# Channel-major projections and gates: three 256-column matmuls into the same PSUM columns, where a 512- and a 256-column one wrote two halves that were added later

## The chip, the core and the metric

The kernel runs on one core of a Trainium2 chip. The metric is the device time of one execution in microseconds. Of three runs before the change the median is 1530.15 us (1529.57 to 1530.34).

The engines that matter are TensorE (PE in the profile; PEld is its weight load), VectorE (DVE), ScalarE (ACT), GpSimd (POOL) and SyncE (SP), which issues most DMAs. A matmul has a stationary operand, loaded ahead of it by a weight load of its own, and a moving operand that streams through column by column; its result is added up in PSUM.

## What is computed

Two layers, each an RMSNorm, one input projection of 2048 features, two mixers side by side (an mLSTM and a gated linear recurrence), and an output projection that is added to x; a last RMSNorm stands at the end. Sequence 256, all in float32. Cut to the parts that the change touches:

```python
u = rms_norm(x, norm_g)
p = u @ w_in
qk, v, o, z_a, ig, fg, xb, z_b = jnp.split(p, SPLIT_AT, axis=-1)
qk = jax.nn.silu(causal_dwconv(qk, qk_conv))
...
xc = causal_dwconv(xb, lru_conv_w) + lru_conv_b
y_b = rg_lru(xc, w_a, b_a, w_x, b_x, lam) * jax.nn.silu(z_b)
...
r = sigmoid(einsum("bshi,hij->bshj", xh, w_a) + b_a)
i = sigmoid(einsum("bshi,hij->bshj", xh, w_x) + b_x)
```

## The kernel before

**Numbers in two parts.** A float32 operand is split into a high part H in a reduced format (fp32r) and the rest L, and a product a b is taken as aH bH + aL bH + aH bL. For the weights, `prepare` does this for every block of 128 x 1024: a ScalarE cast (line 222, tile wH) and a VectorE subtraction (through the helper at line 111, tile wL). The normalised x is kept transposed in x_s as [128, 16 feature tiles, 2 parts, 256 tokens], so that high and low part of one feature tile lie side by side.

**Two forms of projection.** The chunks o, v and z and the output projection are token-major (`mm_a`, lines 238 to 240): stationary is a 128-token slice of x or y, moving is a weight block of 512 columns, three matmuls for the three products into the same PSUM columns. The chunks qk, xb and zb are channel-major (`mm_b`): stationary is a 128 x 128 block of weights, moving is x_s. Here line 255 moves both parts of x_s at once, 512 columns, against wH, so that the product with the high part lands in columns 0 to 255 and that with the low part in columns 256 to 511; line 257 moves the high part against wL and adds into columns 256 to 511. The two halves are added on the way out of PSUM. The gates w_a and w_x (`gate_half`, lines 595 and 597) do the same with xcs, the split output of the convolution.

**On the way out.** `evac_b` copies the first half (ScalarE, line 329), adds the second (VectorE) and multiplies by the norm factor rb (VectorE) into padt (qk, xb: 32 times) or zb (16 times). In the gates ScalarE adds the bias to one half (line 601), VectorE adds the other, and one Sigmoid of 1024 columns follows (line 604).

**Order.** `_plan` lists chunks by layer and group of heads (two layers, four groups). Each chunk is cut into halves of one weight block; the last loop of `tile_trunk` walks over the halves, prepares weights three halves ahead (`AHEAD`), emits the half's matmuls and then pumps background work (convolutions, mLSTM steps, scans) from generators. `pump` stops when its credit is used up; every piece of work takes its estimated cost from the credit, `evac_b` 1.2. A scheduler then settles the order on each engine, by what buffers and operands allow. In PSUM there are two acc tiles of [128, 2, 512] for the projections, and four 512-column buffers (`aux`) that ps_gt (gates), ps_S, ps_n (mLSTM), ps_ty (transposes) and ps_g share. The mLSTM steps use the helper `mm3` (lines 428 to 430), and `gates_mm` (lines 353 and 354) makes the 16 input and forget gate columns into ps_g, once a layer.

Of the kernel before, what the change touches and what calls it, by code (L numbers as in the profile page):

```python
# [9 lines left out]
F32 = mybir.dt.float32  # L10
F32R = mybir.dt.float32r
AF = mybir.ActivationFunctionType
ALU = mybir.AluOpType
# [3 lines left out]
P = 128  # L17
D = 2048
T = 256
# [29 lines left out]
def tile_trunk(ctx, tc, x, xt, par, gw, gb, ws, final_g, out):  # L49
    nc = tc.nc  # L50
    V, S, G, PE = nc.vector, nc.scalar, nc.gpsimd, nc.tensor
# [8 lines left out]
    ps_main = ctx.enter_context(tc.tile_pool(name="ps_main", bufs=2, space=PSUM))  # L60
    ps_aux = ctx.enter_context(tc.tile_pool(name="ps_aux", bufs=4, space=PSUM))

    def aux(name):
        return ps_aux.tile([P, 512], F32, tag="aux", name=name)
# [9 lines left out]
    pars = const.tile([P, DEPTH, NPAR], F32, name="pars")  # L74
# [35 lines left out]
    def tt_(o, a, b, op):  # L110
        return V.tensor_tensor(out=o, in0=a, in1=b, op=op)  # L111

    def stt(o, a, s, b, op0, op1):
        return V.scalar_tensor_tensor(out=o, in0=a, scalar=s, in1=b, op0=op0, op1=op1)

    def ts_(o, a, s1, op0, s2=None, op1=None):
        if s2 is None:
            return V.tensor_scalar(out=o, in0=a, scalar1=s1, scalar2=None, op0=op0)
        return V.tensor_scalar(out=o, in0=a, scalar1=s1, scalar2=s2, op0=op0, op1=op1)

    def log1p_exp_half(x_, tl):
        """returns q with log1p(exp(-|x|)) = 2 q"""
        z = tl("z")
        stt(z, x_, -1.0, x_, ALU.mult, ALU.min)
        S.activation(out=z, in_=z, func=AF.Exp)
        d = tl("d")
        ts_(d, z, 2.0, ALU.add)
        V.reciprocal(out=d, in_=d)
        s = tl("s")
        tt_(s, z, d, ALU.mult)  # L130
        s2 = z
        tt_(s2, s, s, ALU.mult)
        p = d
        ts_(p, s2, 1.0 / 15, ALU.mult)
        for c in (13, 11, 9, 7, 5, 3):
            stt(p, p, 1.0 / c, s2, ALU.add, ALU.mult)
        stt(p, p, 1.0, s, ALU.add, ALU.mult)
        return p
# [47 lines left out]
    halves = []  # L186
    st = {"nload": 0, "credit": 0.0}
# [15 lines left out]
    def add_unit(mms, before=None, after=None):  # L203
        box = {}
        for i in range(2):
            halves.append(dict(box=box, i=i, mm=mms[i], split=None,
                               before=before if i == 0 else None, after=after if i == 1 else None))
# [35 lines left out]
    def mm_b(acc, k0, first, last):  # L243
        def f(H, L):
            Hv = H.rearrange("p (k c) -> p k c", k=4)
            Lv = L.rearrange("p (k c) -> p k c", k=4)
            ps = acc()
            xs = st["x"]
            for k in range(4):
                kt = k0 + k  # L250
                for ct in range(2):
                    csl = slice(P * ct, P * ct + P)
                    s = first and k == 0
                    e = last and k == 3
                    PE.matmul(ps[:, ct, :], Hv[:, k, csl], xs[:, kt].rearrange("p a t -> p (a t)"),  # L255
                              start=s, stop=False, skip_group_check=True)
                    PE.matmul(ps[:, ct, T : 2 * T], Lv[:, k, csl], xs[:, kt, 0, :], start=False, stop=e,  # L257
                              skip_group_check=True)
        return f

    def chunk_in(l, kind, g, postfn, beforefn=None):
        def make_acc():
            box = {}

            def acc():
                if "t" not in box:
                    box["t"] = ps_main.tile([P, 2, 512], F32, tag="acc", name="acc")
                return box["t"]
            return acc

        if kind in ("qk", "xb", "zb"):
            for s_ in range(2):
                acc = make_acc()
                for u in range(2):
                    mms = [mm_b(acc, 8 * u + 4 * i, u == 0 and i == 0, u == 1 and i == 1) for i in range(2)]
                    add_unit(mms, after=(lambda acc=acc, s_=s_: postfn(acc(), s_)) if u == 1 else None)
        else:
            acc = make_acc()
            for u in range(4):
                mms = [mm_a(acc, lambda: st["x"][:, :, 0], lambda: st["x"][:, :, 1], 4 * u + 2 * i,  # L280
                            u == 0 and i == 0, u == 3 and i == 1) for i in range(2)]
                add_unit(mms, before=beforefn if u == 0 else None,
                         after=(lambda: postfn(acc())) if u == 3 else None)

    def bc(ap2, n):
        return ap2.unsqueeze(1).to_broadcast([P, n, T])
# [39 lines left out]

    def evac_b(l, o, acc):
        require(("rb", l))
        S.copy(out=o, in_=acc[:, :, 0:T])
        tt_(o, o, acc[:, :, T : 2 * T], ALU.add)  # L330
        tt_(o, o, bc(st["rb", l], 2), ALU.mult)
        st["credit"] -= 1.2

    def evac_pad(l, acc):
        padt = work.tile([P, 2, 260], F32, tag="pad", name="padt", bufs=2)
# [21 lines left out]
    def gates_gen(l):  # L357
# [13 lines left out]
        tt_(gi, gi, t_, ALU.add)  # L371
        yield 0.6
        q = log1p_exp_half(x_, sc)
        yield 4
        ts_(q, q, -2.0, ALU.mult)
# [207 lines left out]
    def gate_half(l, g, which):  # L583
        def f(H, L):
            xc, xs = st["xc", l, g]
            Hv = H.rearrange("p (b c) -> p b c", b=4)
            Lv = L.rearrange("p (b c) -> p b c", b=4)
            o_t = work.tile([P, 4, T], F32, tag="sA" if which == 0 else "sB", name=f"gate{which}")
            for b in range(2):
                for j in range(2):  # L590
                    ps = aux("ps_gt")
                    jl = slice(P * j, P * j + P)
                    for i in range(2):
                        ib = 2 * b + i
                        PE.matmul(ps, Hv[:, ib, jl], xs[:, ib].rearrange("p a t -> p (a t)"), start=i == 0,  # L595
                                  stop=False, skip_group_check=True)
                        PE.matmul(ps[:, T : 2 * T], Lv[:, ib, jl], xs[:, ib, 0, :], start=False, stop=i == 1,  # L597
                                  skip_group_check=True)
                    ct = 2 * b + j
                    off = (O_BA if which == 0 else O_BX) + 4 * g + ct  # L600
                    S.activation(out=o_t[:, ct, :], in_=ps[:, T : 2 * T], func=AF.Identity,
                                 bias=pars[:, l, off : off + 1])
                    tt_(o_t[:, ct, :], o_t[:, ct, :], ps[:, 0:T], ALU.add)
            st["sig"] = S.activation(out=o_t, in_=o_t, func=AF.Sigmoid)
            st["gate", which] = o_t
        return f

# [239 lines left out]
    for item in _plan():  # L847
        if item[0] == "in":
            emit_in(*item[1:])
        elif item[0] == "gate":  # L850
            _, l, g = item
# [21 lines left out]

# [1 line left out]
def _units():  # L875
    """the weight blocks in the order in which the kernel streams them: two halves a unit"""
    sl = lambda a, n: slice(a, a + n)
    units = []

    def chunk(l, kind, g):  # L880
        if kind in ("qk", "xb", "zb"):
            for s in range(2):
                if kind == "qk":
                    cs = [sl(256 * g + 128 * s, 128), sl(1024 + 256 * g + 128 * s, 128)]
                else:
                    cs = [sl((C_XB if kind == "xb" else C_ZB) + 512 * g + 256 * s, 256)]
                for u in range(2):
                    units.append([("w_in", l, (sl(1024 * u + 512 * i, 512), cs)) for i in range(2)])
        else:
            cs = [sl({"v": C_V, "o": C_O, "z": C_Z}[kind] + 512 * g, 512)]  # L890
            for u in range(4):
                units.append([("w_in", l, (sl(512 * u + 256 * i, 256), cs)) for i in range(2)])

    def out(l, g, c):
        for src in range(2):
            units.append([("w_out", l, (sl(2048 * src + 512 * g + 256 * i, 256), [sl(512 * c, 512)]))
                          for i in range(2)])

    for item in _plan():
        if item[0] == "in":  # L900
            chunk(*item[1:])
        elif item[0] == "gate":
            _, l, g = item
            units.append([(w, l, sl(2 * g, 2)) for w in ("w_a", "w_x")])
        elif item[0] == "out":
            out(*item[1:])
        else:
            _, l, g = item
            for kp in range(4):
                rows = sl(2048 * (kp // 2) + 512 * g + 256 * (kp % 2), 256)  # L910
                for c in (0, 2):
                    units.append([("w_out", l, (rows, [sl(512 * (c + i), 512)])) for i in range(2)])
    return units
# [52 lines left out]
```

## Time and profile before

| | |
|---|---|
| median of three runs | 1530.15 us |
| span of the profiled execution, first to last instruction | 1528.4 us |
| mean granted TensorE clock | 0.997 |
| VectorE, casts' subtractions (line 111, wL) | 643.8 us busy, 529 instructions |
| ScalarE, casts (line 222, wH) | 554.0 us busy, 529 instructions |
| mean DMA rate | 188 GB/s |

Times of the profile belong to one profiled execution, and count from its first instruction; its span is the time that the profile has for it, and the runs' times include a little more around it. A row of a group gives line, engine, operation, tiles (out<-in), shapes and count, then the busy time in us, the mean ns of one, and the idle time of the engine before them. A row of the timeline gives the start and the duration in us, then the same names. A duration of a matmul or a weight load reaches into the next one's.

### The profile page before, as it was taken

To read this page: it belongs to the slowest core of one execution; us is meant where nothing else is said; L and a number is where in the kernel's file an instruction comes from. 1 tells how busy PE (TensorE), PEld (TensorE's weight loads), DVE (VectorE), ACT (ScalarE), POOL (GpSimd) and SP (SyncE) were. 2 spreads that over 40 slices of the span, in tenths; PEclk is the share of its full clock that TensorE was granted. 3 is DMA by queue.
4 is the path that set the end of the run, shared out by engine and by line. 5 is a ranking of instruction groups with operands and counts; after the bars stand their busy time and mean duration, and the time that the engine had idled before them with its cause. 6 is when DMAs were issued, how large, how long until landed. Compare 5 with 4: busy or idle time off the path is not lost.

```text
span 1528.4 us, 19659 instructions
## 1 busy us (share of the span) xinstructions
PE 1510.9 (99%) x7576; PEld 1278.2 (84%) x7576; DVE 1127.6 (74%) x1594; ACT 885.4 (58%) x1141; POOL 37.6 (2%) x109
## 2 busy tenths in 40 slices
PE   8999999999999999999999999999999999999997
PEld 6888888888888888888888888888888888888885
DVE  6888867794677847778658787777847887478874
ACT  7567654674547645575555485557544575444854
POOL 0000100000000000000000001000000000000002
PEclk9999999999999999999999999999999999999998
DMA  9554655455554555445555555545555455555562
GB/s 344 192 188 164 212 185 182 173 196 194 188 190 171 191 193 193 175 183 193 175 184 180 190 176 193 193 173 192 193 193 185 173 184 197 187 182 187 171 223 102
DMA packets 45117, 288.03 MB, mean 188 GB/s; under 512 B 5072, under 2 KB 7648, under 8 KB 11744
## 3 DMA queue, kind: packets, MB, share of 16 engines
q1 hardware_dynamic: 43600, 283.40, 52.4%
q0 software_dynamic: 992, 3.16, 0.7%
q8 instruction: 59, 0.97, 0.3%
q14 instruction: 34, 0.28, 0.1%
q10 hardware_dynamic: 432, 0.23, 0.0%
HBM read 284.66 MB, written 2.11 MB: 188 GB/s over the span
## 4 chain that ended last, share of the span: by engine, by line
PE 98%; ACT 1%; DMA 0%; DVE 0%; SPq 0%; issue 0%; ACTq 0%
PE acc L255 24%; PE acc L238 18%; PE acc L240 18%; PE acc L239 18%; PE acc L257 12%; PE ps_gt L595 2%; PE ps_gt L597 1%; PE acc L788 0%; PE acc L790 0%; PE acc L789 0%; PE ps_ty L551 0%; DMA raw<-in_ws_dram 0%; PE acc_x L790 0%; PE acc_x L788 0%; PE acc_x L789 0%; PE ps_n L428 0%
## 5 line engine op out<-in xcount | busy, mean ns | idle before, releaser
L222 ACT CAST wH<-raw 128x1024 fp32r<-128x1024 f32 (+1 forms) x529 | 554.0, 1049 | 567.6 <-PE acc L240 282.6
L111 DVE TENSOR_TENSOR wL<-raw,wH 128x1024 fp32r<-128x1024 f32 (+1 forms) x529 | 643.8, 1220 | 312.3 <-ACT wH L222 311.5
L255 PE MATMUL acc<-x_s,wH 128*128 128x512 f32 x1536 | 544.1, 399 | 0.0
L257 PE MATMUL acc<-x_s,wL 128*128 128x256 f32 x1536 | 431.2, 281 | 0.0
L255 PEld LDWEIGHTS acc<-x_s,wH 128*128 128x128 f32 x1536 | 288.6, 188 | 71.0
L238 PE MATMUL acc<-wH,x_s 128*128 128x512 f32 x768 | 301.0, 392 | 6.7 <-ACT wH L222 6.7
L239 PE MATMUL acc<-wL,x_s 128*128 128x512 f32 x768 | 300.2, 391 | 0.3 <-DVE wL L111 0.3
L240 PE MATMUL acc<-wH,x_s 128*128 128x512 f32 x768 | 299.8, 390 | 0.0
L257 PEld LDWEIGHTS acc<-x_s,wL 128*128 128x128 f32 x1536 | 290.1, 189 | 0.9
L238 PEld LDWEIGHTS acc<-wH,x_s 128*128 128x128 f32 x768 | 144.7, 188 | 36.2 <-ACT wH L222 6.7
L239 PEld LDWEIGHTS acc<-wL,x_s 128*128 128x128 f32 x768 | 144.7, 188 | 30.3 <-DVE wL L111 1.2
L240 PEld LDWEIGHTS acc<-wH,x_s 128*128 128x128 f32 x768 | 144.6, 188 | 30.1
L238 PE MATMUL acc<-wH,ybH 128*128 128x512 f32 x224 | 88.1, 393 | 0.0
L238 PE MATMUL acc<-wH,yaH 128*128 128x512 f32 x224 | 87.8, 392 | 0.0
L239 PE MATMUL acc<-wL,yaH 128*128 128x512 f32 x224 | 87.4, 390 | 0.0
L240 PE MATMUL acc<-wH,yaL 128*128 128x512 f32 x224 | 87.4, 390 | 0.0
L240 PE MATMUL acc<-wH,ybL 128*128 128x512 f32 x224 | 87.3, 390 | 0.0
L239 PE MATMUL acc<-wL,ybH 128*128 128x512 f32 x224 | 87.2, 389 | 0.0
L238 PEld LDWEIGHTS acc<-wH,yaH 128*128 128x128 f32 x224 | 42.0, 188 | 9.1
L240 PEld LDWEIGHTS acc<-wH,yaL 128*128 128x128 f32 x224 | 42.1, 188 | 8.9
L240 PEld LDWEIGHTS acc<-wH,ybL 128*128 128x128 f32 x224 | 42.0, 188 | 8.8
L238 PEld LDWEIGHTS acc<-wH,ybH 128*128 128x128 f32 x224 | 42.1, 188 | 8.4
(201 smaller groups left out, 1437.2 us busy)
## 6 DMA issues: line engine op xcount, KB each, us to landing
raw<-in_ws_dram SPq DMA_DIRECT2D x260, 1024.0 KB, 4.8
raw<-in_ws_dram SPq DMA_DIRECT2D x6, 512.0 KB, 7.9
xp<-in_xt_dram SPq DMA_DIRECT2D x8, 256.0 KB, 7.4
x_acc<-in_x_dram SPq DMA_DIRECT2D x4, 512.0 KB, 9.7
nb<-nG_d POOLq DMA_DIRECT2D x8, 256.0 KB, 3.7
out_dram<-x_acc SPq DMA_DIRECT2D x8, 256.0 KB, 3.0
raw<-in_ws_dram SPq DMA_DIRECT2D x4, 256.0 KB, 6.3
fg<-in_final_g_dram POOLq DMA_DIRECT2D x2, 512.0 KB, 4.5
```

The source lines that it names most:

```text
L111: return V.tensor_tensor(out=o, in0=a, in1=b, op=op)
L222: S.copy(out=H[:, o : o + w], in_=r[:, o : o + w])
L238: PE.matmul(ps[:, t, :], a_H[:, kt, tsl], Hv[:, k, :], start=s, stop=False)
L239: PE.matmul(ps[:, t, :], a_H[:, kt, tsl], Lv[:, k, :], start=False, stop=False)
L240: PE.matmul(ps[:, t, :], a_L[:, kt, tsl], Hv[:, k, :], start=False, stop=e)
L255: PE.matmul(ps[:, ct, :], Hv[:, k, csl], xs[:, kt].rearrange("p a t -> p (a t)"), start=s, stop=False, skip_group_check=True)
L257: PE.matmul(ps[:, ct, T : 2 * T], Lv[:, k, csl], xs[:, kt, 0, :], start=False, stop=e, skip_group_check=True)
L595: PE.matmul(ps, Hv[:, ib, jl], xs[:, ib].rearrange("p a t -> p (a t)"), start=i == 0, stop=False, skip_group_check=True)
L597: PE.matmul(ps[:, T : 2 * T], Lv[:, ib, jl], xs[:, ib, 0, :], start=False, stop=i == 1, skip_group_check=True)
```

## The change

In `mm_b` and `gate_half` the matmul of 512 columns is cut in two of 256, and all three write to the same 256 columns. The two channel tiles of a chunk, which had a PSUM bank each, share one, so only the very first matmul into the bank clears it. `evac_b` multiplies straight from PSUM. In the gates a buffer holds two channel tiles, and the Sigmoid takes its input from PSUM with the bias. The cost that `evac_b` takes from the credit goes from 1.2 to 0.7.

```diff
@@ mm_b
-                    PE.matmul(ps[:, ct, :], Hv[:, k, csl], xs[:, kt].rearrange("p a t -> p (a t)"),
-                              start=s, stop=False, skip_group_check=True)
-                    PE.matmul(ps[:, ct, T : 2 * T], Lv[:, k, csl], xs[:, kt, 0, :], start=False, stop=e,
-                              skip_group_check=True)
+                    o = ps[:, ct, :]
+                    PE.matmul(o, Hv[:, k, csl], xs[:, kt, 0, :], start=s and ct == 0, stop=False, skip_group_check=True)
+                    PE.matmul(o, Hv[:, k, csl], xs[:, kt, 1, :], start=False, stop=False, skip_group_check=True)
+                    PE.matmul(o, Lv[:, k, csl], xs[:, kt, 0, :], start=False, stop=e, skip_group_check=True)
@@ chunk_in
+        def make_acc_b():
+            box = {}
+
+            def acc():
+                if "t" not in box:
+                    t = ps_main.tile([P, 2, 512], F32, tag="acc", name="acc")
+                    box["t"] = t[:, 0, :].rearrange("p (a t) -> p a t", a=2)
+                return box["t"]
+            return acc
+
...
-                acc = make_acc()
+                acc = make_acc_b()
@@ evac_b
-        S.copy(out=o, in_=acc[:, :, 0:T])
-        tt_(o, o, acc[:, :, T : 2 * T], ALU.add)
-        tt_(o, o, bc(st["rb", l], 2), ALU.mult)
-        st["credit"] -= 1.2
+        tt_(o, acc, bc(st["rb", l], 2), ALU.mult)
+        st["credit"] -= 0.7
@@ gate_half
+                ps = aux("ps_gt").rearrange("p (j t) -> p j t", j=2)
                 for j in range(2):
-                    ps = aux("ps_gt")
                     jl = slice(P * j, P * j + P)
                     for i in range(2):
                         ib = 2 * b + i
-                        PE.matmul(ps, Hv[:, ib, jl], xs[:, ib].rearrange("p a t -> p (a t)"), start=i == 0,
-                                  stop=False, skip_group_check=True)
-                        PE.matmul(ps[:, T : 2 * T], Lv[:, ib, jl], xs[:, ib, 0, :], start=False, stop=i == 1,
+                        o = ps[:, j, :]
+                        PE.matmul(o, Hv[:, ib, jl], xs[:, ib, 0, :], start=i == 0 and j == 0, stop=False,
                                   skip_group_check=True)
+                        PE.matmul(o, Hv[:, ib, jl], xs[:, ib, 1, :], start=False, stop=False, skip_group_check=True)
+                        PE.matmul(o, Lv[:, ib, jl], xs[:, ib, 0, :], start=False, stop=i == 1, skip_group_check=True)
+                for j in range(2):
                     ct = 2 * b + j
                     off = (O_BA if which == 0 else O_BX) + 4 * g + ct
-                    S.activation(out=o_t[:, ct, :], in_=ps[:, T : 2 * T], func=AF.Identity,
-                                 bias=pars[:, l, off : off + 1])
-                    tt_(o_t[:, ct, :], o_t[:, ct, :], ps[:, 0:T], ALU.add)
-            st["sig"] = S.activation(out=o_t, in_=o_t, func=AF.Sigmoid)
+                    st["sig"] = S.activation(out=o_t[:, ct, :], in_=ps[:, j, :], func=AF.Sigmoid,
+                                             bias=pars[:, l, off : off + 1])
```

On TensorE, the first matmuls of the first qk chunk of the first layer; acc is the PSUM tile of the chunk, wH and wL are the two parts of the weights. Before:

```order
L255 MATMUL acc<-x_s,wH 128x512
L257 MATMUL acc<-x_s,wL 128x256
L255 MATMUL acc<-x_s,wH 128x512
L257 MATMUL acc<-x_s,wL 128x256
L255 MATMUL acc<-x_s,wH 128x512
L257 MATMUL acc<-x_s,wL 128x256
```

And after the change, at the same place:

```order
L256 MATMUL acc<-x_s,wH 128x256
L257 MATMUL acc<-x_s,wH 128x256
L258 MATMUL acc<-x_s,wL 128x256
L256 MATMUL acc<-x_s,wH 128x256
L257 MATMUL acc<-x_s,wH 128x256
L258 MATMUL acc<-x_s,wL 128x256
```

A pair has become a triple; over the whole program TensorE's matmuls grow by 1536 in the projections and 128 in the gates.

On TensorE, in the gates of the second group of heads of the first layer, between the first and the second gate's matmuls before; ps_gt is the gates' PSUM buffer, xcs the split convolution output, and yaH and yaL are the parts of the mLSTM result that the output projection reads:

```order
L597 MATMUL ps_gt<-xcs,wL 128x256
L238 MATMUL acc<-wH,yaH 128x512
L239 MATMUL acc<-wL,yaH 128x512
L240 MATMUL acc<-wH,yaL 128x512
L238 MATMUL acc<-wH,yaH 128x512
L595 MATMUL ps_gt<-xcs,wH 128x512
L597 MATMUL ps_gt<-xcs,wL 128x256
```

And after the change, at the end of the gates of that group:

```order
L607 MATMUL ps_gt<-xcs,wL 128x256
L604 MATMUL ps_gt<-xcs,wH 128x256
L606 MATMUL ps_gt<-xcs,wH 128x256
L607 MATMUL ps_gt<-xcs,wL 128x256
L238 MATMUL acc<-wH,yaH 128x512
L239 MATMUL acc<-wL,yaH 128x512
```

Before, matmuls of the output projection stood between the gate matmuls in two places of each group; now all 48 gate matmuls of the group stand together and the output projection follows them.

On VectorE, where the first qk half of the first layer is taken out of PSUM; padt is the padded input of the convolution, rb the norm factor. Before:

```order
L118 TENSOR_SCALAR sc_d<-sc_s 8x256
L111 TENSOR_TENSOR padt<-padt,acc 128x2x256
L111 TENSOR_TENSOR padt<-padt,rb 128x2x256
L111 TENSOR_TENSOR wL<-raw,wH 128x1024
L114 SCALAR_TENSOR_TENSOR qc<-padt,pars,qc 128x256 x4
```

And after the change:

```order
L114 SCALAR_TENSOR_TENSOR sT<-sc_i,gbs,sc_z 8x256
L111 TENSOR_TENSOR padt<-acc,rb 128x2x256
L391 SCALAR_TENSOR_TENSOR sc_s<-sT 8x256
L111 TENSOR_TENSOR wL<-raw,wH 128x1024
```

The add from acc is gone, and the multiply by rb reads acc itself.

## The prediction

> **What bounds the kernel now.** I read the engines' busy shares first, then the chain that ended last, then what TensorE waited for, and last the start times of single matmuls.
>
> ```profile
> PE 1510.9 (99%) x7576; PEld 1278.2 (84%) x7576; DVE 1127.6 (74%) x1594; ACT 885.4 (58%) x1141; POOL 37.6 (2%) x109
> PE 98%; ACT 1%; DMA 0%; DVE 0%; SPq 0%; issue 0%; ACTq 0%
> PE acc L238 <- ACT wH L222: 6.7, 1, 6.7
> PE acc L239 <- DVE wL L111: 0.3, 1, 0.3
> ```
>
> The first row gives busy time per engine, the second the shares of the chain that ended last, and the last two are all that the view of waits has for the matmul rows (total us, times, longest). TensorE (PE) waited twice, for 7.0 us in all, while the first weights were being loaded and split. The rest of the chain, 98% of 1528.4 us, is TensorE passing from one matmul to the next. VectorE (DVE) is busy for 74% and ScalarE (ACT) for 58%, beside it. So a change is worth what it does to the spacing of the matmuls; work taken from DVE and ACT alone is worth nothing unless PE was waiting for it.
>
> A matmul's own duration does not serve, since its row overlaps the next. The spacing does: start to start, over a block of known length.
>
> ```profile
> L255 PE MATMUL acc<-x_s,wH 128*128 128x512 f32 x1536 | 544.1, 399 | 0.0
> L595 PE MATMUL ps_gt<-xcs,wH 128*128 128x512 f32 x128 | 45.8, 393 | 0.0
> 157.24 0.39 PE L255 MATMUL acc<-x_s,wH 128*128 128x512 f32 x1
> 157.46 0.28 PE L257 MATMUL acc<-x_s,wL 128*128 128x256 f32 x1
> 157.57 0.40 PE L255 MATMUL acc<-x_s,wH 128*128 128x512 f32 x1
> ...
> 179.84 0.40 PE L238 MATMUL acc<-wH,x_s 128*128 128x512 f32 x1
> 294.00 0.40 PE L595 MATMUL ps_gt<-xcs,wH 128*128 128x512 f32 x1
> ...
> 296.80 0.39 PE L238 MATMUL acc<-wH,yaH 128*128 128x512 f32 x1
> 599.65 0.39 PE L240 MATMUL acc<-wH,yaL 128*128 128x512 f32 x1
> ...
> 605.77 0.40 PE L240 MATMUL acc<-wH,ybL 128*128 128x512 f32 x1
> ```
>
> The two group rows give the counts: 1536 pairs in the projections (L255 with L257), 128 in the gates (L595 with L597). The timeline rows begin with the start in us. From 157.24 to 179.84 stands one chunk, 8 halves of 8 pairs, 64 pairs with nothing between: 22.60 us / 64 = **353.1 ns for a pair**. The gate block from 294.00 to 296.80 has 8 pairs: **350.0 ns**. From 599.65 to 605.77 stand 27 matmuls of 512 columns in a row (token-major loop): **226.7 ns each**.
>
> **The change, part by part.**
>
> *The matmuls.* Each pair (512 and 256 columns) becomes three matmuls of 256. The columns that stream through TensorE stay 768; what is new is a third weight load and a third start. So the term is 1536 x (3s - 353.1 ns) + 128 x (3s - 350.0 ns), s being the spacing of a 256-column matmul in an unbroken run. Before has such runs elsewhere:
>
> ```profile
> 606.00 0.28 PE L428 MATMUL ps_S<-qks 128*128 128x256 f32 x1
> ...
> 606.36 0.22 PE L428 MATMUL ps_S<-qks 128*128 128x128 f32 x1
> 621.06 0.28 PE L428 MATMUL ps_n<-vH,PH 128*128 128x258 f32 x1
> ...
> 621.77 0.40 PE L255 MATMUL acc<-x_s,wH 128*128 128x512 f32 x1
> 796.02 0.28 PE L353 MATMUL ps_g<-x_s,gwp 128*104 128x256 f32 x1
> ...
> 799.81 0.40 PE L238 MATMUL acc<-wH,x_s 128*128 128x512 f32 x1
> ```
>
> In ps_S three matmuls take 0.36 us (120 ns each); in ps_n six of 258 columns take 0.71 us (118.3); in ps_g 32 take 3.79 us (118.4). All three accumulate into the same PSUM columns over and over, as the changed loops will, and each matmul has a weight load of its own. ps_g is by far the longest, but its stationary side has 104 columns instead of 128; ps_n has 128 and agrees. I take s = 118.35 ns, the middle of these two. Then 3s = 355.05; projections +1.95 x 1536 = **+3.0 us**, gates +5.05 x 128 = **+0.6 us**, together **+3.6 us**.
>
> The bounds of s. Above, 120 ns of ps_S: 360 ns a triple, +10.6 and +1.3, so +11.9 us. Further up, a full price for a split: 512 columns cost 226.7 alone, twice 118.35 are 236.7, +10.0 ns at 1664 places, +16.6 us. That is more than the sum above because the pair today costs 353.1 and not 226.7 + 118.35 = 345.05: it already pays 8 ns that the separate runs do not show. Whether they go with the mixture of sizes, as I take it, or stay with these loops, no row decides. Below, the closest that any weight loads follow each other in these stretches:
>
> ```profile
> L255 PEld LDWEIGHTS acc<-x_s,wH 128*128 128x128 f32 x1536 | 288.6, 188 | 71.0
> 606.36 0.19 PEld L429 LDWEIGHTS ps_S<-qks 128*128 128x128 f32 x1
> 606.47 0.19 PEld L430 LDWEIGHTS ps_S<-qks 128*128 128x128 f32 x1
> 606.58 0.19 PEld L238 LDWEIGHTS acc<-wH,ybH 128*128 128x128 f32 x1
> ```
>
> These belong to 128-column matmuls, and their starts are 0.11 us apart (0.22 us over two). At s = 112, which is that pace with the rounding, a triple is 336: -17.1 x 1536 and -14.0 x 128, -28.1 us. Nothing in the trace runs 256 columns that fast, so I stay with the longer runs.
>
> *Copies and adds removed.* Each of the 48 evacuations (32 into padt, 16 into zb) loses a ScalarE copy and a VectorE add; the multiply stays and reads PSUM instead. In the gates the Identity with bias becomes the Sigmoid, so 64 adds and 16 wide Sigmoids go.
>
> ```profile
> L329 ACT COPY padt<-acc 128x512 f32<-128x512 f32 x32 | 18.5, 579 | 0.0
> L111 DVE TENSOR_TENSOR padt<-padt,acc 128x512 f32<-128x512 f32 x32 | 21.8, 680 | 0.0
> L111 DVE TENSOR_TENSOR padt<-padt,rb 128x512 f32<-128x512 f32 x32 | 22.2, 694 | 0.9
> L601 ACT ACTIVATE gate<-ps_gt,pars 128x256 f32<-128x256 f32 x64 | 26.9, 477 | 2.6 <-PE ps_gt L597 2.6
> L111 DVE TENSOR_TENSOR gate<-gate,ps_gt 128x256 f32<-128x256 f32 x64 | 24.7, 413 | 8.4 <-ACT gate L601 8.4
> L604 ACT ACTIVATE gate<-gate 128x1024 f32<-128x1024 f32 x16 | 17.0, 1061 | 0.0
> ```
>
> At the padt durations for all 48, DVE loses 48 x 0.680 + 64 x 0.413 = 59 us, ACT 48 x 0.579 + 16 x 1.061 = 45 us. The multiply from PSUM is bounded by the 680 ns of the add that reads PSUM today and its own 694; a Sigmoid of 256 columns by the 477 of the Identity and a quarter of 1061 below it. All of it lies beside matmuls, and PE was waiting for none of it: 0 us. Were that cover gone, it would have been worth at most those 59 us; the cover is the matmul stream itself.
>
> *What moves.* The smaller credit (0.7 for 1.2) lets the background work start earlier, so ps_S stands 12 matmuls further ahead, and the gate's matmuls, which needed eight ps_gt buffers out of four and so were broken up by out-projection matmuls, need four and stand together. No DMA moves on a queue: the weights' loads follow the casts in the same order. The one wait this can touch:
>
> ```profile
> 129.14 0.39 PE L239 MATMUL acc<-wL,x_s 128*128 128x512 f32 x1
> 129.59 0.39 PE L428 MATMUL ps_n<-vH,PH 128*128 128x258 f32 x1
> ```
>
> Here, and once in the second layer, ps_n starts 0.45 us after a matmul that takes 0.227: 0.2 us lost, since PH came late behind ScalarE's casts. After the change nearly the same rows stand there, and it may be lost again. Bounds are -0.5 us (both go) and +1.9 us (what is queued behind waits for four gate buffers, and those for four Sigmoids of 0.477 us). I take 0, the nearest row being a wait of 0.2 us. What would be late next is PE itself.
>
> Sum: 1528.4 us (the span of the profiled execution) + 3.6 = 1532.0. The median of the runs, 1530.15, stands 1.75 above that span; carried over unchanged, 1533.7 us, 0.24% slower. About 0.2%, 3.1 us, is what a measurement of this kernel can tell from no change. In terms of s: below 117.0 ns the change is faster by more than that, above 118.2 slower; my value lies just over that edge.
>
> **The rivals.**
>
> *A split costs its full price* (slower). The 8 ns that the pair pays beyond its separate runs belong to these loops (their operands, their PSUM) and stay: +10.0 ns at 1664 places, 1546.8 us. For it: nothing shows that the mixture causes them, and the gate pairs, mixed in the same way, pay 5 instead of 8. Against it: ps_g, fed from the same x_s, runs at 118.4 over 32. It decides from s = 118.4 upward; at 121 it is there in full.
>
> *The uniform run is no dearer than the pair* (no change). s lies between 117.0 and 118.2, the third matmul hides in today's 8 ns, and the relief of DVE and ACT buys nothing: 1530.2 +- 3.1. For it: my s stands 0.15 ns over that edge. Against it: all three runs are at 118.3 or more.
>
> *Weight loads set the pace* (faster). At 112 ns a triple is cheaper than a pair: 1502 us. For it: loads do follow each other that closely. Against it: they do so only under 128-column matmuls.
>
> *Weight loads cannot overlap* (slower). The loads become the bound: 7576 + 1664 = 9240 loads of 188 ns are 1737 us, more than the whole span. Against it: the rows above start 0.11 us apart while each is 0.19 long, so they overlap. The Trainium skill (Perfetto Trace Analysis, section Identifying the Most-Contended Engine) speaks for this rival: it judges TensorE by the busy share of LDWEIGHTS rather than of matmuls, and by that measure the change raises the fuller resource by a fifth. The trace agrees only in part: that share is 84% now, but it is a sum of rows that overlap.
>
> *The change does nothing of what it says*: the adds do go, by the diff. That they buy no time is in the second rival.
>
> **How the numbers follow.** Forecast (s from 118.2 to 119.8): 0.40, its own range 1533 to 1541. Full price: 0.12. No change: 0.33. Loads at 112 or some way towards it: 0.13. Loads that do not overlap: 0.02. So faster 0.13, same 0.33, slower 0.54. The predicted time is the forecast's, 1533.7. The range takes in the forecast, no change and the full price, 0.85 together: from 1527 (the edge of no change) to 1548 (just above 1546.8); it takes in the +11.9 of ps_S and leaves out the 112 ns.
>
> **What would show it.** Right: in an unbroken stretch of triples the spacing is 118 to 119 ns, the blocks of 512 keep 226.7, PE waits for no more than the 7 us of the start, and DVE's busy time is some 59 us lower, ACT's some 45, with the span no shorter. Wrong: triples at 360 and more (full price) or well under 350 (the pace of the loads); waits of PE for ps_gt or the Sigmoids in the gates; or a shorter span with unchanged spacing, which would mean that DVE or ACT did hold PE in a way that the waits do not show.

## The result and the profile after

| | before | after |
|---|---|---|
| median of the runs | 1530.22 us (1529.57 to 1530.34) | 1541.49 us (1541.22 to 1542.03) |
| span of the profiled execution | 1528.4 us | 1539.7 us |
| granted TensorE clock | 0.997 | 0.998 |

The change makes the kernel slower: the ratio to before is 1.0076, with a 95% interval of 1.0061 to 1.009. That is 11.3 us, and the spans differ by the same 11.3.

The page of the changed kernel has these rows: busy time by engine, and the shares of the chain that ended last by engine.

```profile
PE 1522.9 (99%) x9240; PEld 1368.0 (89%) x9240; DVE 1081.4 (70%) x1482; ACT 845.8 (55%) x1075; POOL 38.8 (3%) x109
PE 98%; ACT 1%; DMA 0%; DVE 0%; SPq 0%; issue 0%; ACTq 0%
```

DVE lost 46 us of busy time and ACT 40, and the chain is still 98% TensorE. The view of waits has one row for the matmuls, the start of the program:

```profile
PE acc L238 <- ACT wH L222: 6.3, 1, 6.3
```

So no new wait came in. The timeline of TensorE has the same chunk as the prediction's 64 pairs (start in us, duration, line, tiles):

```profile
157.74 0.28 PE L256 MATMUL acc<-x_s,wH 128*128 128x256 f32 x1
157.85 0.28 PE L257 MATMUL acc<-x_s,wH 128*128 128x256 f32 x1
157.97 0.28 PE L258 MATMUL acc<-x_s,wL 128*128 128x256 f32 x1
158.09 0.28 PE L256 MATMUL acc<-x_s,wH 128*128 128x256 f32 x1
...
180.77 0.40 PE L238 MATMUL acc<-wH,x_s 128*128 128x512 f32 x1
```

From 157.74 to 180.77 stand 192 matmuls: 23.03 us against 22.60 before, 120.0 ns each and 359.8 a triple where a pair took 353.1. The kernel has work for 24 such chunks (1536 / 64): 24 x 0.43 = 10.3 us. Fifteen of them stand unbroken in each trace. The first takes 0.1 us more; the other fourteen take 22.60 us before and 23.03 after.

Inside the pair, the rows of before show what the split meets:

```profile
158.29 0.40 PE L255 MATMUL acc<-x_s,wH 128*128 128x512 f32 x1
158.52 0.28 PE L257 MATMUL acc<-x_s,wL 128*128 128x256 f32 x1
158.63 0.40 PE L255 MATMUL acc<-x_s,wH 128*128 128x512 f32 x1
158.87 0.28 PE L257 MATMUL acc<-x_s,wL 128*128 128x256 f32 x1
```

From one start to the next, the matmuls of 512 columns take 0.23 and 0.24 us here and the one of 256 takes 0.11. Over the 64 pairs of the chunk the means are 236.5 and 116.6 ns (from the same rows of the trace, in ns), where matmuls of 512 columns in a row take 226.7 and of 256 in a row 120.0. So splitting the wide matmul (236.5 to 240) costs about 3.4 ns, and the narrow one loses as much, since it no longer stands behind a wide one.

The gates of the group in which the prediction read 350.0 ns, 16 triples:

```profile
295.83 0.28 PE L604 MATMUL ps_gt<-xcs,wH 128*128 128x256 f32 x1
...
301.58 0.39 PE L238 MATMUL acc<-wH,yaH 128*128 128x512 f32 x1
```

5.75 us, 359.4 ns a triple against 350.0 a pair: 128 x 9.4 = 1.2 us. Together 11.5 us, the whole of the 11.3 measured within the rounding of the rows. The matmuls of 512 columns in a row still take 226.7 ns.

### The profile page after: what moved, and what is told of

Read it like the earlier page. It is cut to its first block, busy times and chain, and to the rows that moved or that the text cites. A ratio compares the mean times of both kernels' runs of the same rounds, so it can differ in the third digit from the quotient of the medians.

```text
span 1539.7 us, 22741 instructions
## 1 busy us (share of the span) xinstructions
PE 1522.9 (99%) x9240; PEld 1368.0 (89%) x9240; DVE 1081.4 (70%) x1482; ACT 845.8 (55%) x1075; POOL 38.8 (3%) x109
## 4 chain that ended last, share of the span: by engine, by line
PE 98%; ACT 1%; DMA 0%; DVE 0%; SPq 0%; issue 0%; ACTq 0%
PE acc L238 18%; PE acc L239 18%; PE acc L240 18%; PE acc L256 12%; PE acc L258 12%; PE acc L257 12%; PE ps_gt L606 1%; PE ps_gt L607 1%; PE ps_gt L604 1%; PE acc L798 0%; PE acc L796 0%; PE acc L797 0%; PE ps_ty L559 0%; PE acc_x L798 0%; PE acc_x L796 0%; PE acc_x L797 0%
## 5 line engine op out<-in xcount | busy, mean ns | idle before, releaser
L256 PE MATMUL acc<-x_s,wH 128*128 128x256 f32 x1536 | 434.9, 283 | 0.0
L257 PE MATMUL acc<-x_s,wH 128*128 128x256 f32 x1536 | 434.6, 283 | 0.0
L256 PEld LDWEIGHTS acc<-x_s,wH 128*128 128x128 f32 x1536 | 294.7, 192 | 1.0
L257 PEld LDWEIGHTS acc<-x_s,wH 128*128 128x128 f32 x1536 | 294.8, 192 | 0.9
L258 PEld LDWEIGHTS acc<-x_s,wL 128*128 128x128 f32 x1536 | 294.7, 192 | 0.0
```

The costliest lines, as they stand in the source:

```text
L256: PE.matmul(o, Hv[:, k, csl], xs[:, kt, 0, :], start=s and ct == 0, stop=False, skip_group_check=True)
L257: PE.matmul(o, Hv[:, k, csl], xs[:, kt, 1, :], start=False, stop=False, skip_group_check=True)
L258: PE.matmul(o, Lv[:, k, csl], xs[:, kt, 0, :], start=False, stop=e, skip_group_check=True)
```

## The experiments

The measure in all of them is this one chunk, first start to the start behind it, beside the time of the kernel. Before has 22.60 us there, the changed kernel 23.03.

**1. Only the split** (`e1_split_only`, from before):

```diff
-                    PE.matmul(ps[:, ct, :], Hv[:, k, csl], xs[:, kt].rearrange("p a t -> p (a t)"),
-                              start=s, stop=False, skip_group_check=True)
+                    PE.matmul(ps[:, ct, 0:T], Hv[:, k, csl], xs[:, kt, 0, :], start=s, stop=False, skip_group_check=True)
+                    PE.matmul(ps[:, ct, T : 2 * T], Hv[:, k, csl], xs[:, kt, 1, :], start=False, stop=False,
+                              skip_group_check=True)
...
-                        PE.matmul(ps, Hv[:, ib, jl], xs[:, ib].rearrange("p a t -> p (a t)"), start=i == 0,
-                                  stop=False, skip_group_check=True)
+                        PE.matmul(ps[:, 0:T], Hv[:, ib, jl], xs[:, ib, 0, :], start=i == 0, stop=False,
+                                  skip_group_check=True)
+                        PE.matmul(ps[:, T : 2 * T], Hv[:, ib, jl], xs[:, ib, 1, :], start=False, stop=False,
+                                  skip_group_check=True)
```

> Before's kernel with only the 512-column matmul cut in two of 256 (projections and gates); the PSUM halves, the copy, the add and the Sigmoid stay as before. Theory weight load: a 256-column matmul with a 128-column weight load of its own is spaced 120 ns wherever it writes, so a triple is 360 ns and the time that of the changed kernel, 1541.5 us +- 1. Rival same columns: the last 1.7 ns of each (120.05 against 118.35) come from adding three times in a row into the same PSUM columns; here two of the three write to columns that the one ahead of them did not, triples come to 356 to 358 and the time to 1535 to 1538. Rival relief: the removed copies and adds were worth something in the changed kernel; then this one is slower than 1542.5.

Measured: 1541.87 us (1541.74 to 1542.23), ratio to before 1.0079 (1.0064 to 1.0094). Its busy times from the page, and then the first start of the chunk and the start behind it from the timeline:

```profile
PE 1523.0 (99%) x9240; PEld 1367.7 (89%) x9240; DVE 1130.4 (73%) x1594; ACT 882.1 (57%) x1139; POOL 37.9 (2%) x109
```

```profile
158.48 0.28 PE L255 MATMUL acc<-x_s,wH 128*128 128x256 f32 x1
...
181.51 0.40 PE L238 MATMUL acc<-wH,x_s 128*128 128x512 f32 x1
```

23.03 us, to the hundredth what the changed kernel has, with DVE and ACT as busy as before. So the split alone makes the whole loss. That all three write to the same PSUM columns does not matter: that rival falls. All the rest of the change, the copies and adds among it, is worth 0.4 us by the medians (1541.87 against 1541.49), and the ranges overlap, so this is not clear of the scatter.

**2. Fewer columns, fewer weights.** Four runs cut the size of the projection matmuls of the changed kernel, but for the first feature tile of each accumulation (12 of the chunk's 192). With n tokens or m weight columns:

```diff
-                    PE.matmul(o, Hv[:, k, csl], xs[:, kt, 0, :], start=s and ct == 0, stop=False, skip_group_check=True)
+                    m, n = (P, T) if s else (104, 224)
+                    cs = slice(P * ct, P * ct + m)
+                    o = ps[0:m, ct, 0:n]
+                    PE.matmul(o, Hv[:, k, cs], xs[:, kt, 0, 0:n], start=s and ct == 0, stop=False, skip_group_check=True)
...
```

`e3_moving224` has n = 224 and m = 128, `e4_stationary104` n = 256 and m = 104, `e8_both_smaller` both (the diff shows it), `e9_moving240` n = 240 and m = 128, `e10_stationary116` n = 256 and m = 116; the other two matmuls of the triple are cut alike.

> The changed kernel whose projection matmuls move only 224 of the 256 tokens, but for the first feature tile of each accumulation; the last 32 tokens of the projections lack most of their sum. Theory weight load: the pace is that of the 128-column weight load, triples stay at 360 ns and the time within 1 us of the changed kernel. Rival streaming: the columns set the pace, a matmul loses 32/256 of some 107 ns, 13 ns, the triples come to 320 and the time to some 1482 us (1536 x 3 x 7/8 matmuls, 13 ns each, less 54).

> The changed kernel whose projection matmuls load only 104 of the 128 weight columns, but for the first feature tile of each accumulation; 24 of every 128 channels lack most of their sum. Theory weight load: the load is shorter, the pace falls to the 118 ns of the ps_g run (104 columns), triples come to 354 to 355 and the time 7 to 8 us lower, 1533 to 1535. Rival streaming or same columns: triples stay at 360, 1541.5 us.

The first and the last start of the chunk in both, e3 ahead of e4:

```profile
155.18 0.28 PE L257 MATMUL acc<-x_s,wH 128*128 128x256 f32 x1
...
176.70 0.40 PE L238 MATMUL acc<-wH,x_s 128*128 128x512 f32 x1
```

```profile
158.07 0.28 PE L259 MATMUL acc<-x_s,wH 128*128 128x256 f32 x1
...
180.79 0.40 PE L238 MATMUL acc<-wH,x_s 128*128 128x512 f32 x1
```

With 224 tokens the chunk takes 21.52 us, 112.1 ns a matmul, and the kernel 1505.94 us (one run). That is neither the 120 of the theory nor the 107 of the rival. (The rival's sum counts 7/8 of the matmuls as narrowed, 4032; the edit narrows 15 of 16, 4320. The same slip is in the third expectation below, where 4320 would give 1478 us.) With 104 weight columns it takes 22.72 us, 118.3 ns, and the kernel 1535.29 (one run): the spacing that the theory said, a time 0.3 us above its range, and the very spacing that ps_g showed before the change. The weight loads of e3, starts in us:

```profile
157.91 0.19 PEld L258 LDWEIGHTS acc<-x_s,wH 128*128 128x128 f32 x1
158.02 0.19 PEld L259 LDWEIGHTS acc<-x_s,wL 128*128 128x128 f32 x1
158.13 0.19 PEld L257 LDWEIGHTS acc<-x_s,wH 128*128 128x128 f32 x1
...
158.58 0.19 PEld L258 LDWEIGHTS acc<-x_s,wH 128*128 128x128 f32 x1
```

Six loads from 157.91 to 158.58, 0.112 us apart, each row being 0.19 long. The loads are even to the nanosecond (111 or 112) while the starts of the matmuls scatter from 109 to 114, which reads as loads waiting for loads. That would make two floors, one set by the loads and one by the columns. This was put to the test by taking both down:

> The changed kernel with 104 weight columns and 224 tokens in the projection matmuls, but for the first feature tile; part of the channels and tokens lacks most of its sum. Theory two floors: with 128 weight columns the loads follow each other at 111.7 ns at the closest, and the 224 columns alone would be faster; with 104 weight columns that floor lies at about 92, and 224 columns take 118.4 less 32/256 of 107, 105 ns; triples 315, time 1535 less 4032 x 13.3 = 1482 us. Rival: 111.7 is what 224 columns take whatever the load; then the time stays at 1505.

```profile
154.53 0.28 PE L258 MATMUL acc<-x_s,wH 128*128 128x256 f32 x1
...
174.75 0.40 PE L238 MATMUL acc<-wH,x_s 128*128 128x512 f32 x1
```

20.22 us for the 192, 1479.02 us for the kernel (one run). Leaving out the 12 matmuls of full size, at 118 ns, the rest come to (20220 - 12 x 118) / 180 = 104.5 ns. So 112 is not what 224 tokens need: it goes with loading 128 columns, and with 104 the same tokens take 104.5. That half of the expectation holds. The other half, that the columns alone set 104.5 and 118.3, no run separates from the loads. What remained was why 256 tokens with 128 weight columns take 120.0 when both, 112 and 118.3, are lower:

> The changed kernel with 240 of 256 tokens moving in the projection matmuls, but for the first feature tile; the last 16 tokens lack most of their sum. Seen so far: columns alone (104 weight columns) 118.4 ns at 256 and 104.5 at 224, so 111.4 at 240; loads of 128 columns 111.7. Theory larger of the two: 111.7 to 112, time 1541.5 - 4320 x 8.2 = 1506 us, as at 224. Theory near collision: where the two floors lie close together each matmul pays 1 to 2 ns more, 113 to 114, 1510 to 1515 us.

> The changed kernel with 116 of 128 weight columns in the projection matmuls, but for the first feature tile; 12 of every 128 channels lack most of their sum. Theory near collision: the load floor falls by 12/128 of 107, to 102, far enough below 118.4: spacing 118.4 as with 104 columns, 1535 us. Theory of a price by weight column: halfway between 118.4 and 120.0, 119.2, 1538.5 us.

```profile
155.27 0.28 PE L257 MATMUL acc<-x_s,wH 128*128 128x256 f32 x1
...
176.86 0.39 PE L238 MATMUL acc<-wH,x_s 128*128 128x512 f32 x1
```

```profile
157.03 0.28 PE L259 MATMUL acc<-x_s,wH 128*128 128x256 f32 x1
...
179.46 0.40 PE L238 MATMUL acc<-wH,x_s 128*128 128x512 f32 x1
```

With 240 tokens (1509.20 us) the chunk's 21.59 us come to 112.0 for the 180 narrower ones ((21590 - 12 x 119) / 180): the pace of the loads and no more, although the two floors are then closest together. So a collision of the two is not it. The time is 3 us above the 1506 expected, partly for another reason: six of the fifteen unbroken chunks take 21.9 us, with one stop of 0.3 us, and the view of waits has six waits of a weight load of these triples for VectorE's subtraction (line 111, wL). With both sizes cut (`e8_both_smaller`) it has seven, 3.0 us in all. For the changed kernel it has none in the triples: VectorE begins to count only when the matmuls get shorter. With 116 weight columns (1527.59 us) 22.43 us, 116.8 ns, less than with 104. Neither theory gives that: 118.3, 116.8 and 120.0 at 104, 116 and 128 are not in order of the load. It also shows that 118.3 is no floor of 256 columns. The last 1 to 3 ns of a spacing stay unexplained.

**3. The sizes sorted.** Today's pair costs more than its two sizes in runs of their own, 226.7 and 120.0. Whether that is the alternation was tried on before's kernel, with the same matmuls into the same columns in another order:

```diff
-            for k in range(4):
-                kt = k0 + k
-                for ct in range(2):
...
+            for k in range(4):
+                for ct in range(2):
+                    PE.matmul(ps[:, ct, :], Hv[:, k, P * ct : P * ct + P], xs[:, k0 + k].rearrange("p a t -> p (a t)"),
+                              start=first and k == 0, stop=False, skip_group_check=True)
+            for k in range(4):
+                for ct in range(2):
+                    PE.matmul(ps[:, ct, T : 2 * T], Lv[:, k, P * ct : P * ct + P], xs[:, k0 + k, 0, :], start=False,
+                              stop=last and k == 3, skip_group_check=True)
```

> Before's projections with the eight 512-column matmuls of a half first and its eight 256-column ones after them; same matmuls, same columns, gates as before. Theory weight load: an alternating pair pays 8 ns more than its sizes do in runs of their own because of the alternation; sorted, a half costs 8 x 226.7 + 8 x 120 = 2774 ns instead of 2825, 347 a pair, -10 us, 1520 +- 2 us. Rival: the 8 ns belong to these loops (weights as the stationary side, x_s as the moving one); then the halves stay at 2825 and the time at 1530.

Measured: 1523.12 us (1522.34 to 1523.29), ratio 0.9955 (0.9938 to 0.9971): faster than before, by 6.8 us of the 10 expected. The chunk's two ends, and the runs of eight at its start, from the timeline:

```profile
156.31 0.39 PE L251 MATMUL acc<-x_s,wH 128*128 128x512 f32 x1
...
158.13 1.11 PE L255 MATMUL acc<-x_s,wL 128*128 128x256 f32 x8
159.08 0.40 PE L251 MATMUL acc<-x_s,wH 128*128 128x512 f32 x1
...
160.92 0.28 PE L255 MATMUL acc<-x_s,wL 128*128 128x256 f32 x1
...
178.63 0.40 PE L238 MATMUL acc<-wH,x_s 128*128 128x512 f32 x1
```

22.32 us, 348.8 ns a pair instead of 353.1. The alternation does cost, and the rival that ties it to the loop's operands falls. What is left over 346.7 sits where the sizes change. The first eight wide matmuls, which follow other wide ones, take 1.82 us; the next eight, behind narrow ones, 1.84. Their starts are 234, 235, 229, 232, 231, 227, 226 and 227 ns apart, so the price is spread over five matmuls, 27 ns in all. The first narrow one behind a wide one takes 113 ns instead of 120, which gives 7 back. If that were a fixed price a change, longer runs should save more of it and shorter ones less. Three orders tried it; in `e5_zigzag` every second half starts with its narrow matmuls, and in the other two the loops over k go in steps of two or of one:

```diff
+            for part in ((narrow, wide) if k0 // 4 % 2 else (wide, narrow)):
+                part(range(4))
...
+            for k in (0, 2):
+                wide((k, k + 1))
+                narrow((k, k + 1))
...
+            for k in range(4):
+                wide((k,))
+                narrow((k,))
```

> As the kernel with wide matmuls first, but every second half of a chunk begins with its 256-column matmuls, so that most runs of one size are 16 long instead of 8. Theory transition: each change from a run of 256 columns back to one of 512 costs about 18 ns over 226.7 and 120 (read from the kernel with runs of 8: 2792 ns a half against 8 x 346.7 = 2774); runs of 16 give 346.7 + 18 / 16 = 347.8 a pair, 1536 x -5.3 = -8 us, 1522 +- 1 us. Rival: the sorted kernel's gain came from elsewhere, and longer runs add nothing: 1523 or more.

> Before with the matmuls of a half in runs of four 512-column and four 256-column ones. Theory transition, 18 ns a change of size back: 346.7 + 4.5 = 351.2 a pair, -3 us, 1527 +- 1. Rival: only the alternation of single matmuls is dear; then runs of 4 are as good as runs of 8, 349 a pair, 1523.

> Before with runs of two 512-column and two 256-column matmuls. Theory transition with a fixed price: 346.7 + 9 = 355.7 a pair, dearer than the alternation, +4 us, 1534. Rival, a price that cannot pass that of the alternation (6.4 a pair): 353 a pair at most, 1530 or less.

The two ends of the chunk, for runs of 16 and then for runs of 2:

```profile
156.15 0.39 PE L252 MATMUL acc<-x_s,wH 128*128 128x512 f32 x1
...
178.42 0.39 PE L238 MATMUL acc<-wH,x_s 128*128 128x512 f32 x1
```

```profile
157.10 0.39 PE L252 MATMUL acc<-x_s,wH 128*128 128x512 f32 x1
...
179.38 0.40 PE L238 MATMUL acc<-wH,x_s 128*128 128x512 f32 x1
```

| run length | chunk | a pair | wide, narrow (mean to the next start) | time | ratio to before |
|---|---|---|---|---|---|
| 1 (before) | 22.60 us | 353.1 ns | 236.5, 116.6 ns | 1530.0 us | |
| 2 | 22.28 | 348.1 | 233.0, 115.2 | 1522.86 (one run) | |
| 4 | 22.43 | 350.5 | 231.9, 118.5 | 1526.32 | 0.9977 (0.9967 to 0.9986) |
| 8 | 22.32 | 348.8 | 229.7, 119.1 | 1523.12 | 0.9955 (0.9938 to 0.9971) |
| 16 | 22.27 | 348.0 | 228.4, 119.6 | 1521.70 | 0.9946 (0.9931 to 0.9961) |

(For the runs of 4, the matmuls from 156.76 to 179.19.) At 16 and at 4 the fixed price gives the measured time within 1 us, at 2 it is wrong by 11 us and with the wrong sign, and the rival's bound holds there without saying why. So the theory of a fixed price falls. The two means show why the order is uneven. A wide matmul gets steadily cheaper as the runs get longer, roughly as a price would have it that is spread over the first five after a change. A narrow one is cheapest in runs of 2 and dearer in longer ones, so in runs of 2 a cheap narrow one meets a wide one that is already cheaper than in alternation. What makes either price is not shown; that single alternating matmuls are the dearest order of the five is. Of the kernels that compute the whole result, the runs of 16 are the fastest, faster than before and than the changed kernel.

## Why the prediction was right, and where its size was off

**The bound.** Right: TensorE, and nothing else. Busy time taken from DVE and ACT (46 and 40 us; 59 and 45 were worked out) bought nothing clear of the scatter, which experiment 1 shows by giving it back. The stall ahead of ps_n stayed too.

```profile
129.51 0.39 PE L239 MATMUL acc<-wL,x_s 128*128 128x512 f32 x1
129.96 0.39 PE L436 MATMUL ps_n<-vH,PH 128*128 128x258 f32 x1
```

0.45 us again, as the term of 0 had it.

**The form of the sum.** Right: 1536 and 128 times the triple less the pair gives 11.5 us, the gates being 1.2 of it, where the spans differ by 11.3.

**The size of s.** This term was off: "I take s = 118.35 ns, the middle of these two". Measured are 120.0 in the projections, so +6.7 ns a triple and not +1.95, and in all 11.3 us and not 3.6. By the prediction's own signs, "118 to 119 ns" did not come; 359.8 a triple is all but the "360 and more" that it named as a sign against itself. The measured 1541.49 us lies just above the 1533 to 1541 that it gave the forecast alone, and inside the whole range only because this takes in ps_S and the full price.

The two runs that it trusted more misled for different reasons. ps_g is long, but has 104 weight columns, and experiment 2 gives the projections the same 118.3 as soon as they have 104 too. ps_n has 128, but is only six long, and what it takes depends on what stands ahead of it. The same six matmuls in the changed kernel, first start and the start behind them:

```profile
625.72 0.28 PE L436 MATMUL ps_n<-vH,PH 128*128 128x258 f32 x1
...
626.44 0.28 PE L256 MATMUL acc<-x_s,wH 128*128 128x256 f32 x1
```

In ns, the six take 723 here, 120.5 each, and 712 before, 118.7 each. All six such blocks of either trace agree within 1 ns. The instructions are the same; before the change alternating pairs stand ahead of them, after it a run of 256-column matmuls. In the kernel with runs of eight narrow matmuls ahead of them they take 723 or 724 as well. So the 118.3 was in part that of the alternation ahead of it, which an unbroken run of triples does not have. It is not the whole: six of the eight blocks of nine ps_n matmuls behind wide ones take 118.0 ns each in both kernels, and why they stay below 120 no run shows. The projections' long runs with 128 weight columns stand at 120.0 both in the changed kernel and in experiment 1. Such a run was not in the trace of before.

The upper bound, 120 ns from ps_S, gives +11.9, close to the 11.3, but this is luck: its rows are read to 0.01 us, so 0.36 us over three matmuls leaves 117 to 123 open, and in ns they are 357, 119.0 each. For the same reason the choice of the forecast over no change was finer than its evidence. It rested on 118.35 against an edge of 118.2, while 0.71 us over six matmuls is known to some 1.7 ns each; ps_g is known to 0.3 ns, but has the smaller weight block. That the kernel would get slower came out right; that it was told from no change was in part luck.

**The rivals.** The full price (+16.6) did not come, since the alternating pair was dear by itself (a wide matmul takes 236.5 ns in it, not 226.7), and experiment 3 shows that most of this goes when the sizes are kept apart. That the third matmul hides in it fell as well: it hides in part only, 6.7 ns a triple being left. The loads do set a pace, but at 112 ns, and it shows only with 240 columns or fewer; 256 never ran that fast in a steady run (116.8 at the least). Loads that cannot overlap are refuted again by e3, 0.112 us apart and 0.19 long. The Trainium skill's rule (Perfetto Trace Analysis, section Identifying the Most-Contended Engine), to judge how near TensorE is to its limit by the busy share of LDWEIGHTS, beside the share of peak FLOPs, pointed the right way here: 84% to 89%, and slower. The 84% that the prediction read is not "a sum of rows that overlap", though: it is the time in which at least one load runs, 1278.2 us before and 1368.0 after, 7% more. The sum of the rows, by which that section defines the share, is 1420 us before and 1751 after, the fifth that was forecast, and 114% of the span: rows that overlap, so that it measures no room that is left. And the kernel of runs of eight is faster than before at the same 84%, as its page of the profile shows, so that share alone does not tell.

```profile
PE 1504.5 (99%) x7576; PEld 1280.1 (84%) x7576; DVE 1129.4 (74%) x1594; ACT 886.0 (58%) x1141; POOL 38.6 (3%) x109
```

## What to carry to other kernels

Where TensorE is the whole chain, price an edit by start-to-start spacing over a long block, not by the durations of rows, and take the price from a block that has the same weight columns, the same moving columns and the same sizes ahead of it, and is long enough that a hundredth of a microsecond does not decide. Work moved off VectorE and ScalarE was worth nothing here, where no matmul waited for it, and one wide matmul was worth keeping even though its result had to be added later on an engine with time to spare. Where two sizes alternate, try them sorted: here that alone was worth 0.5%, with no instruction added or removed.

## What the runs showed of the hardware that was not expected

For these fp32r matmuls the spacing is 104.5 ns at 224 moving columns and 118.3 at 256 with 104 weight columns, and 226.7 at 512 with 128; with 128 weight columns and 224 or 240 moving ones it is 112, the even pace of the loads. The order of the sizes matters (353.1 ns a pair in alternation, 348 to 350.5 in runs of 2 to 16). A wide matmul behind narrow ones takes up to 241 ns instead of 226.7, and the extra is spread over about five of them; a narrow one behind a wide one takes 113 instead of 120. So a short block carries the marks of what stands ahead of it: the same six matmuls of 258 columns took 712 ns behind alternating pairs and 723 behind a run of 256-column ones. A narrower weight block does not act evenly: 120.0, 116.8 and 118.3 ns at 128, 116 and 104 columns. These prices were seen; what makes them was not shown.
